# Two Strassen pairs in place of four plain output-gate blocks, and silu and the forget gate by other ScalarE functions, in a sparse-attention and gated-recurrence layer

## The chip, the core and the metric

The kernel runs on one core of a Trainium2 chip. The metric is the device time of one execution in microseconds (us); the time before is the median of three executions. All data is float32; products are made on TensorE (PE) out of high and low parts.

## The reference

One residual block over 512 tokens and 16 learned meta tokens, model width 2048. All projections come from one weight matrix `w_in` (2048 x 12368):

```
h = rms_norm(x, norm_g);  proj = h @ w_in
q_a, k_a, v_a, z_a, q_i, k_i, w_i, q_b, f_b, i_b, z_b, gates = split(proj)
# branch A: sparse attention: indexer scores, top-k keys per query, attention over them
o_a = dsa_attention(q, k, v, qi, ki, wi, chunk_ids, topk)
y_a = o_a * silu(z_a)
# branch B: gated linear recurrence, 8 heads
qb = silu(q_b);  f = lbh + (1 - lbh) * sigmoid(f_b)
o_b = rms_norm(hgrn2_chunkwise(qb, 1 - f, i_b, log(f)))
y_b = o_b * silu(z_b)
out = x + sum_n(sigmoid(gates)_n * (y_n @ w_branch_n)) @ w_out
```

## The kernel before

The program is recorded in Python: each helper of `Core` (L47 on) issues one instruction and moves a clock of its engine by an estimated cost (these clocks only decide the order). `E.tt` (L108) is a VectorE (DVE) operation on two tensors, `E.act` (L102) one on ScalarE (ACT), `E.dma_add` (L117) a DMA that adds into its target, issued by GpSimd (POOL). What is not a big product is written as generators ("tasks"). `pump` (L226) is called between matmuls and lets a task issue its next step when its operands should be ready and the clocks of DVE and ACT stand no further ahead of PE's than a limit; tasks of priority 5 or more (the top-k search and the mask table) have a limit of 1.2 us. The order on each engine is thereby fixed when the program is built, and each engine works its list in that order.

A weight tile `raw` (128x1024) comes by DMA and is split into `wh`, its rounding made on ACT, and `wl` = `raw` - `wh`, made on DVE (`hi_lo`, L399). Each product is three matmuls: high x high, high x low, low x high. There are 6 buffers for `raw` and 3 for `wh` and `wl`.

The order of the big products:

- **Class stage**: the indexer's key block, eight indexer query blocks (128 columns each), and `NZA` = 8 output-gate blocks of attention, z_a (`jobs`, L1560 on). A block is 2048 deep: 16 x 3 matmuls with 512 moving columns into the bank `pg`. Beside them run the indexer's tasks (`score`, `rl`), `tops_task` (L1199: sums of the activations for Strassen, the tiles `tr`, `t3` and `tT`), the top-k search (L679: `MAX` and `MATCH_REPLACE`, 64 rounds in all) and the mask table (`CAST`). In the last block `place_t3` (L1231) puts eight of the sums in the place of activations that were read, by an ACT copy to `hH` and a DVE difference to `hL` each.
- **Pairs**: two blocks of 128 columns are made together by Strassen's scheme with seven products (`SEVEN`, L326; `run_pair`, L1264). A product is 8 x 3 matmuls with 256 moving columns (272 in two of them where the meta tokens are needed), in the banks `px`, `py`, `px`, `pv`, `pz`, `pw`, `pz`. A pair splits 7 weight tiles; the three sums of its weights are two DVE additions `raw<-raw,raw` and two adding DMAs; six DVE operations on `p` and `r` put the two results together. The results `r0` and `r1` are finished one or two products later (`fin`). The order is 16 pairs for the recurrence (each head: forget gate with query, then value with output gate), 8 for attention, 16 for the merge gates. Beside them run one recurrence task after another (eight heads; bank `phl`, tiles `QA`, `hk`, `TT`, `attn`), and then the attention tasks.
- **Branch and output stages** follow from about 1200 us; the change leaves them as they are.

What a result waits for too long is stored to DRAM (`held`) and fetched again by a DMA that ACT issues. A z_a block is stored to `zd` and fetched as `zs` at the end of its attention head.

silu is made by a Sigmoid on ACT and a multiplication on DVE: `silu_mul` (L1112) for the blocks of the class stage, `silu` (L1136) for the recurrence's query (`qg`) and output gate (`zg`). The forget gate is a Sigmoid, then one ACT instruction that scales and shifts by the table `lbt`.

Of the kernel before, what the change touches and what calls it, by code (L numbers as in the profile page):

```python
# [12 lines left out]
AF = mybir.ActivationFunctionType  # L13
# [24 lines left out]
LAT = 180.0  # L38
SAME = {"pe": 0.0, "act": 60.0, "dve": 125.0, "pool": 60.0}
MARGIN = 300.0  # L40
NZA = 8
NSLOT = 71
ORDER = (1, 0)
LIMIT = 2000.0
# [141 lines left out]
def hybrid_kernel(ctx, tc, x, meta, vecs, w_in, rows, w_branch, w_out,  # L186
# [39 lines left out]
    def pump(limit=3000.0):  # L226
        moved = True
        while moved:
            moved = False
            for t in list(tasks):  # L230
                now = E.clk["pe"]
                lim = limit if t.prio < 5 else 1200.0
                if t.t + MARGIN <= now and E.clk["dve"] < now + lim and E.clk["act"] < now + limit:
                    if not t.done and t.step():
                        moved = True
                        break
# [235 lines left out]
    def consts():  # L472
        yield E.clk["pe"] + 3000.0
        l0, l1 = cvec[:, 16:24], cvec[:, 24:32]
        E.tt(lbt[:, :, 0], l0, l1, OP.max)
        E.tt(lbt[:, :, 1], l0, lbt[:, :, 0], OP.subtract)
        E.tt(lbt[:, :, 2], l1, lbt[:, :, 0], OP.subtract)
        yield E.act(lbt[:, :, 1:3], lbt[:, :, 1:3], AF.Exp)
        E.tt(lbt[:, :, 3], lbt[:, :, 1], lbt[:, :, 2], OP.add)
        E.dve([lbt], [lbt], 8, lambda v: v.reciprocal(lbt[:, :, 3], lbt[:, :, 3]))  # L480
        E.tt(lbt[:, :, 0], lbt[:, :, 1], lbt[:, :, 3], OP.mult)
        yield E.ts(lbt[:, :, 1], lbt[:, :, 0], -1.0, 1.0, OP.mult, OP.add)
        E.dve([gq1], [cvec], 2, lambda v: v.tensor_copy(gq1, cvec[:, 32:34]))
        E.dve([gq1], [], 2, lambda v: v.memset(gq1[0:32, :], 1.0))
        for t, o, nb in ((tabQ, 64, 4), (tabK, 128, 5)):
            E.tt(t[:, :, 0:32], tabA[:, :nb, 0:32], RB[:, None, o:o + 32].to_broadcast([128, nb, 32]), OP.mult)
            E.tt(t[:, :, 32:64], tabA[:, :nb, 32:64], RB[:, None, o + 32:o + 64].to_broadcast([128, nb, 32]),
                 OP.mult)
# [301 lines left out]
    def spill(to, s, e, n=512):  # L790
        yield e
        nc.sync.dma_start(to[:, :n], s[:, :n])
        S.put(s)
# [315 lines left out]
        yield e  # L1109


    def silu_mul(b, name):  # L1112
        s = slot(name)
        E.act(s[:, :512], b, AF.Sigmoid)
        E.tt(s[:, :512], b, s[:, :512], OP.mult)
        B1.put(b)
        return s

    def d_kiwi(b):
        s = slot("kw")  # L1120
        E.act(s[:80, :272], b[:80, 0, :272], AF.Copy)
# [11 lines left out]

    ka_tasks, va_tasks, qa_tasks, hg_tasks = {}, {}, [], []

    def silu(s, name):  # L1136
        t = slot(name)
        E.act(t[:, :512], s[:, :512], AF.Sigmoid)
        E.tt(s[:, :512], s[:, :512], t[:, :512], OP.mult)
        S.put(t)  # L1140
        return E.wr[s.tensor.name][0]

    def d_za(h):
        def f(b):
            s = silu_mul(b, "zs")
            spawn(spill(zd[h], s, E.wr[s.tensor.name][0]), 0)
        return f

    def r_za(h):
        return lambda s: spawn(spill(zd[h], s, silu(s, "zg")), 0)  # L1150

    def r_ka(g):
        def f(s):
# [11 lines left out]
    def r_qb(h):  # L1165
        def f(s):
            if h == 0:
                spawn(lb_task(), 1)
            silu(s, "qg")
            hg.setdefault(h, {})["q"] = hold(s, 512)  # L1170
        return f

# [11 lines left out]

    def r_zb(h):
        def f(s):
            silu(s, "zg")
            hg[h]["z"] = hold(s, 512)
        return f

# [63 lines left out]
    def lack_bank(n=1):  # L1254
        z = 0
        while len(B1.free) < n:
# [4 lines left out]
            if len(B1.free) < n:  # L1261
                E.clk["pe"] += 200

    def run_pair(pr, nxt, late, last):  # L1264

        bk, W, m, t = {}, slice(0, 256), pr.meta, {}
# [23 lines left out]
        for i, (wn, tn, bn, on_) in enumerate(SEVEN):  # L1290
            op = pr.ops[i]
            split_upto(op["prep"] + 2)
            if not on_:
                lack_bank()
                bk[bn] = B1.get("p" + bn)
            wide = m if bn == "x" else 0
            b = bk[bn][:, :256 + wide]
            need[0] = (2, 1, 1, 2, 1, 1, 2)[i]
            keep[0] = (2, 1, 1, 1, 1, 1, 1)[i]
            for k in range(8):  # L1300
                th, tl = TB[k][tn + "m" if wide else tn]
                st_ = k == 0 and not on_
                E.mm(b, op["h"][k], th, st_, False, loose=True)
                E.mm(b, op["h"][k], tl, False, False, loose=True)
                E.mm(b, op["l"][k], th, False, k == 7, loose=True)
                if k == WHEN:
                    flush()
                    if i == 0:
                        sum_w(pr, "s2")
                        sum_w(pr, "s1")  # L1310
                pump(LIMIT)
            if i in combine:
                pend.append(lambda f=combine[i], b=b: f(b))
            elif i == 0:
                lack()
                t["p1"] = slot("p1")
                E.act(t["p1"][:, W], b[:, wide:], AF.Copy)
            state["lazy"] = True
            split_upto(op["prep"] + 3)
            state["lazy"] = False  # L1320
            if i == 0:
                sum_w(pr, "s4")
            elif i == 2:
                lack()
                t["r0"] = slot("r0")
                E.act(t["r0"][:, :256 + m], b, f0)
                B1.put(bk["x"])
                if nxt:
                    sum_w(nxt, "s3")
            if last and i > 4:  # L1330
                flush()
            if late:
                late.pop(0)()
            if i == 5:
                def fin(s=t["r1"], f=f1, d=d1):
                    if f != AF.Copy:
                        E.act(s[:, :512], s[:, :512], f)
                    d(s)
                late.append(fin)
            elif i == 6:  # L1340
                def fin(s=t["r0"], f=f0, d=d0, m=m):
                    if f != AF.Copy:
                        E.act(s[:, m + 256:m + 512], s[:, m + 256:m + 512], f)
                    d(s)
                late.append(fin)
            if last:
                if i == 4:
                    S.put(*hH[:8], *hL[:8], *[t for k in range(8) for t in TB[k]["tiles"][:2]])
                    finish_y(ORDER[0])
# [215 lines left out]
    jobs[nclass0].pre = lambda: mask_t.append(spawn(make_masks(), 5))  # L1565
    jobs[-1].pre = lambda: sum_w(jobs[ji], "s3")
    nclass = len(jobs)
    SG, CP = AF.Sigmoid, AF.Copy
    gates = [(n, j) for n in ORDER for j in range(0, 16, 2)]

    def gate_pair():
        n, j = gates.pop(0)
        c = C_G + D * n + 128 * j
        return c, c + 128, 0, ((CP, r_gate(n, j)), (CP, r_gate(n, j + 1)))

    def za_pair(h):
        c = C_ZA + 128 * h
        return c, c + 128, 0, ((CP, r_za(h)), (CP, r_za(h + 1)))

    def attn_pairs(g):  # L1580
        return [(C_KA + 128 * g, C_QA + 256 * g, NM, ((CP, r_ka(g)), (CP, r_qa(2 * g)))),
                (C_VA + 128 * g, C_QA + 256 * g + 128, NM, ((CP, r_va(g)), (CP, r_qa(2 * g + 1))))]

    def hgrn_pairs(h):
        return [(C_FB + 128 * h, C_QB + 128 * h, NM, ((SG, r_fb(h)), (CP, r_qb(h)))),
                (C_IB + 128 * h, C_ZB + 128 * h, NM, ((CP, r_ib(h)), (CP, r_zb(h))))]

    order = [za_pair(h) for h in range(NZA, 8, 2)]
# [84 lines left out]
    for ji, job in enumerate(jobs[2:], 3):  # L1673
# [34 lines left out]
        for ch in job.chunks:  # L1708
            split_upto(ch["prep"] + 2)
            for kk_ in range(ch["nk"]):  # L1710
                kt = ch["k0"] + kk_
                if job.kind == "in":
                    mh, ml = hH[kt], hL[kt]
                else:
                    mh, ml = yH[job.n, kt], yL[job.n, kt]
                for o, c in parts:
                    mm3(o, ch, kk_, kt, mh[:, c], ml[:, c], kt == 0, kt == job.kts - 1)
                pump()
            if ji == nclass and ch["k0"] == 0:
                place_t3(0)  # L1720
                place_t3(4)
# [73 lines left out]
```

## Time and profile before

| | |
|---|---|
| time, median of 3 (lowest to highest) | 1546.42 us (1544.67 to 1546.59) |
| profiled execution: its time, its span | 1545.51 us, 1543.7 us |
| first block of the class stage with 512 columns / last four z_a blocks / pairs start | 51 us / 195 to 239 us / 239 us |
| last `MAX` of the top-k search / last `phl` matmul of the recurrence / first matmul of the branch stage | 393.3 us / 701.9 us / 1199.1 us |
| DVE busy, of the stretch from 239 to 400 us; from 400 to 700 us | 149.75 of 160.8 us; 232.75 of 300 us |

The span runs from the first instruction to the last; 1.8 us of the execution's own time lie around it. A busy PE is no PE at its peak: the records of matmuls that follow each other overlap, so what a matmul costs is read from start to start. In the timeline a row is: start, duration, engine, line, operation, tiles (out<-in), shapes, count, and in brackets the idle time of the engine before it with what ended that.

### The profile page before, as it was taken

The numbers are of one execution on the slowest core, as the hardware profiler recorded it, in microseconds if no ns is written. First come the engines' busy times: TensorE is split into PE (matmuls) and PEld (weight loads), VectorE is DVE, ScalarE is ACT, GpSimd is POOL, SyncE is SP. The second block draws the span as 40 slices with busy tenths as digits, with TensorE's granted clock in tenths as the row PEclk, the third lists the DMA queues.
The fourth block names the chain that finished last, engine by engine and source line by source line (L and its number), as shares of the span: only waits on it lengthen the run. The fifth ranks groups of instructions, "written<-read, shape, count | busy, mean of one in ns | idle before, by whom it ended". The sixth has DMA issues, their size and how long they took to land. (4 is left out here: it accounts for less than half of the span.)

```text
span 1543.7 us, 30244 instructions
## 1 busy us (share of the span) xinstructions
PE 1514.8 (98%) x12312; PEld 1425.1 (92%) x12312; DVE 1156.2 (75%) x1954; ACT 689.4 (45%) x1049; POOL 160.7 (10%) x170
## 2 busy tenths in 40 slices
PE   7999999999999999999999999999999999999998
PEld 6888889999999999999999999998999788889998
DVE  6799988999788778877776776875876444768665
ACT  5565424444443444334455455454454433434332
POOL 3100001010000101001110110110110000002221
PEclk9999999999999999999999999999999999999999
DMA  9323354787675757675775766767767664448883
GB/s 263 82 69 82 103 142 106 175 187 171 172 177 147 182 148 172 157 187 149 181 180 156 191 163 180 185 156 179 170 159 193 213 201 131 154 121 214 213 213 95
DMA packets 305563, 251.72 MB, mean 163 GB/s; under 512 B 11732, under 2 KB 266208, under 8 KB 305424
## 3 DMA queue, kind: packets, MB, share of 16 engines
q1 hardware_dynamic: 279120, 180.33, 40.1%
q0 software_dynamic: 13888, 50.42, 19.0%
q10 hardware_dynamic: 12416, 19.04, 3.9%
q8 instruction: 96, 1.57, 0.4%
q14 instruction: 43, 0.35, 0.1%
HBM read 169.90 MB, written 29.52 MB: 129 GB/s over the span
## 5 line engine op out<-in xcount | busy, mean ns | idle before, releaser
L103 ACT ACTIVATE wh<-raw 128x1024 fp32r<-128x1024 f32 x398 | 421.5, 1060 | 591.9 <-PE pz L93 137.4
L109 DVE TENSOR_TENSOR wl<-raw,wh 128x1024 fp32r<-128x1024 f32 x396 | 485.1, 1226 | 130.8 <-ACT wh L103 124.7
L118 POOL DMA_DIRECT2D raw<-raw x96 | 83.8, 980 | 1076.0 <-DVE raw L109 613.8
L93 PE MATMUL px<-hH,wh 128*128 128x272 f32 (+1 forms) x640 | 186.9, 292 | 2.7 <-ACT p L103 2.7
L93 PE MATMUL px<-hL,wh 128*128 128x272 f32 (+1 forms) x640 | 182.9, 286 | 0.0
L93 PE MATMUL px<-hH,wl 128*128 128x272 f32 (+1 forms) x640 | 182.8, 286 | 0.0
L93 PE MATMUL po<-wh,mh 128*128 128x256 f32 x896 | 159.3, 281 | 0.5 <-DVE xq L109 0.5
L93 PEld LDWEIGHTS po<-wh,mh 128*128 128x128 f32 x896 | 137.6, 189 | 0.8 <-DVE xq L109 0.7
L93 PE MATMUL po<-wl,mh 128*128 128x256 f32 x448 | 125.8, 281 | 0.0
L93 PEld LDWEIGHTS px<-hH,wh 128*128 128x128 f32 x640 | 120.8, 189 | 3.7 <-ACT p L103 3.1
L93 PE MATMUL pv<-tT,wh 128*128 128x256 f32 x640 | 121.0, 287 | 0.0
L93 PEld LDWEIGHTS px<-hL,wh 128*128 128x128 f32 x640 | 120.8, 189 | 0.0
L93 PEld LDWEIGHTS px<-hH,wl 128*128 128x128 f32 x640 | 120.6, 188 | 0.0
L93 PE MATMUL pz<-tT,wh 128*128 128x256 f32 x640 | 119.4, 286 | 0.0
L109 DVE TENSOR_TENSOR raw<-raw,raw 128x1024 f32<-128x1024 f32 x96 | 117.3, 1221 | 1.6
L93 PE MATMUL pw<-tT,wh 128*128 128x256 f32 x640 | 118.1, 284 | 0.0
L95 PE MATMUL pg<-yH,wh 128*128 128x512 f32 x256 | 101.7, 397 | 1.2 <-ACT yH L103 1.2
L95 PE MATMUL pg<-yL,wh 128*128 128x512 f32 x256 | 101.4, 396 | 1.2 <-DVE yL L109 1.2
L95 PE MATMUL pg<-yH,wl 128*128 128x512 f32 x256 | 101.6, 397 | 0.0
L93 PEld LDWEIGHTS pz<-tT,wh 128*128 128x128 f32 x640 | 99.1, 190 | 0.3
L93 PEld LDWEIGHTS pv<-tT,wh 128*128 128x128 f32 x640 | 98.1, 189 | 0.2
L93 PEld LDWEIGHTS pw<-tT,wh 128*128 128x128 f32 x640 | 97.9, 188 | 0.3
(309 smaller groups left out, 3564.4 us busy)
## 6 DMA issues: line engine op xcount, KB each, us to landing
raw<-in_w_in_dram SPq DMA_DIRECT2D x192, 512.0 KB, 6.0
raw<-raw POOLq DMA_DIRECT2D x96, 512.0 KB, 5.8
raw<-in_w_branch_dram SPq DMA_DIRECT2D x32, 512.0 KB, 4.0
raw<-in_w_out_dram SPq DMA_DIRECT2D x32, 512.0 KB, 6.4
gd<-r SPq DMA_DIRECT2D x32, 256.0 KB, 2.6
gate<-gd SPq DMA_DIRECT2D x32, 256.0 KB, 4.2
held<-r SPq DMA_DIRECT2D x20, 264.0 KB, 2.3
held<-r SPq DMA_DIRECT2D x20, 256.0 KB, 2.0
```

Source lines behind the costliest of these rows:

```text
L93: self.nc.tensor.matmul(out, lhsT, rhs, start=start, stop=stop, skip_group_check=True)
L95: self.nc.tensor.matmul(out, lhsT, rhs, start=start, stop=stop)
L103: self.nc.scalar.activation(out, in_, f, **kw)
L109: self.nc.vector.tensor_tensor(out, a, b, op=op)
L118: self.nc.gpsimd.dma_start(out, a, accum_op=OP.add)
```

## The change

- `NZA` goes from 8 to 4. Output-gate blocks 4 to 7 of attention are no more blocks of the class stage but two Strassen pairs, which stand behind the recurrence's 16 pairs and ahead of attention's.
- silu is one ACT instruction with the function Silu; the 24 multiplications on DVE (8 `zs`, 8 `qg`, 8 `zg`) are gone. For the recurrence's query and output gate the ACT instruction works in place on `r1`; for the new pairs one result is made by Silu straight from the bank, in place of a copy.
- The forget gate is made by Tanh of half the input; the table `lbt` is changed to match (one small DVE operation more).
- In the last block of the class stage `pump` has a limit of 0.5 us in place of 3.0; the limit of low-priority tasks is the smaller of 1.2 us and the caller's.

The diff, cut to its core:

```
-NZA = 8
+NZA = 4
...
-                lim = limit if t.prio < 5 else 1200.0
+                lim = limit if t.prio < 5 else min(limit, 1200.0)
...
-        yield E.ts(lbt[:, :, 1], lbt[:, :, 0], -1.0, 1.0, OP.mult, OP.add)
+        E.ts(lbt[:, :, 1], lbt[:, :, 0], -0.5, 0.5, OP.mult, OP.add)
+        yield E.ts(lbt[:, :, 0], lbt[:, :, 0], 0.5, 0.5, OP.mult, OP.add)
...
-    def silu_mul(b, name):
-        s = slot(name)
-        E.act(s[:, :512], b, AF.Sigmoid)
-        E.tt(s[:, :512], b, s[:, :512], OP.mult)
-        B1.put(b)
-        return s
...
-    def silu(s, name):
-        t = slot(name)
-        E.act(t[:, :512], s[:, :512], AF.Sigmoid)
-        E.tt(s[:, :512], s[:, :512], t[:, :512], OP.mult)
-        S.put(t)
-        return E.wr[s.tensor.name][0]
...
     def d_za(h):
         def f(b):
-            s = silu_mul(b, "zs")
+            s = slot("zs")
+            E.act(s[:, :512], b, AF.Silu)
+            B1.put(b)
             spawn(spill(zd[h], s, E.wr[s.tensor.name][0]), 0)
...
-        return lambda s: spawn(spill(zd[h], s, silu(s, "zg")), 0)
+        return lambda s: spawn(spill(zd[h], s, E.wr[s.tensor.name][0]), 0)
...
+    def silu(o, i):
+        E.act(o, i, AF.Silu)
+
+    def tanh_half(o, i):
+        E.act(o, i, AF.Tanh, scale=0.5)
...
-                E.act(t["r0"][:, :256 + m], b, f0)
+                f0(t["r0"][:, :256 + m], b)
...
-        return c, c + 128, 0, ((CP, r_za(h)), (CP, r_za(h + 1)))
+        return c, c + 128, 0, ((silu, r_za(h)), (silu, r_za(h + 1)))
...
-        return [(C_FB + 128 * h, C_QB + 128 * h, NM, ((SG, r_fb(h)), (CP, r_qb(h)))),
-                (C_IB + 128 * h, C_ZB + 128 * h, NM, ((CP, r_ib(h)), (CP, r_zb(h))))]
-
-    order = [za_pair(h) for h in range(NZA, 8, 2)]
+        return [(C_FB + 128 * h, C_QB + 128 * h, NM, ((tanh_half, r_fb(h)), (silu, r_qb(h)))),
+                (C_IB + 128 * h, C_ZB + 128 * h, NM, ((copy, r_ib(h)), (silu, r_zb(h))))]
+
+    order = []
     for h in range(8):
         order += hgrn_pairs(h)
+    order += [za_pair(h) for h in range(NZA, 8, 2)]
...
-                pump()
+                pump(500.0 if ji == nclass else 3000.0)
```

The joint between the class stage and the first pair, on DVE. The names: `hL_52` is the last of the eight differences of `place_t3`; `wl35`, `wl36`, `wl37` are the low parts of the weights for the second, third and fourth product of the first pair; `zs_252` is the multiplication for the last z_a block; `m8`, `tk` belong to the top-k search. Before:

```order
L109 TENSOR_TENSOR hL_52_406<-t3_229_1992,hH_51_405 128x256
L109 TENSOR_TENSOR wl35_2475<-raw35_2233,wh35_2474 128x1024
L688 MAX m8_120<-tk_234_2005 128x8
L689 MATCH_REPLACE tk_234_2005<-m8_120,tk_234_2005 128x400
L109 TENSOR_TENSOR zs_252_2504<-pg_98_2424,zs_252_2504 128x512
L109 TENSOR_TENSOR wl36_2508<-raw37_2312,wh36_2507 128x1024
L109 TENSOR_TENSOR raw35_2233<-raw35_2233,raw36_2275 128x1024
L109 TENSOR_TENSOR raw34_2196<-raw35_2233,raw34_2196 128x1024
L109 TENSOR_TENSOR wl37_2541<-raw35_2233,wh37_2540 128x1024
```

In the changed program the same place on DVE, where the pair's low parts are `wl26` to `wl32`; first the piece that ends with the low part for the first product:

```order
L109 TENSOR_TENSOR tT_246_2121<-tr_242_2080,tT_245_2120 128x512
L109 TENSOR_TENSOR tT_247_2122<-tr_243_2081,tT_247_2122 128x256
L321 CAST masks_100<-mf_236_2041 128x256
L692 MAX m8_120<-tk_234_2002 128x8
L693 MATCH_REPLACE tk_234_2002<-m8_120,tk_234_2002 128x528
L109 TENSOR_TENSOR wl26_2131<-raw26_1736,wh26_2130 128x1024
```

and then the piece from the last difference on:

```order
L109 TENSOR_TENSOR hL_52_406<-t3_229_1989,hH_51_405 128x256
L109 TENSOR_TENSOR wl27_2181<-raw27_1805,wh27_2180 128x1024
L321 CAST masks_100<-mf_236_2041 128x256
L692 MAX m8_120<-tk_234_2002 128x8
L693 MATCH_REPLACE tk_234_2002<-m8_120,tk_234_2002 128x528
L109 TENSOR_TENSOR wl28_2214<-raw29_1981,wh28_2213 128x1024
L109 TENSOR_TENSOR raw27_1805<-raw27_1805,raw28_1896 128x1024
L109 TENSOR_TENSOR raw26_1736<-raw27_1805,raw26_1736 128x1024
L109 TENSOR_TENSOR wl29_2247<-raw27_1805,wh29_2246 128x1024
```

What moved: the sums of the activations (`tT`), the mask table and the first rounds of the top-k search, which stood two to five blocks ahead of the first pair, now stand in its last block and in the pair itself; between `wl26` and the first `hL` there are two more rounds of mask, `MAX` and `MATCH_REPLACE`. The multiplication `zs` is gone.

The recurrence's pairs, on DVE, at the end of a forget-gate and query pair and the start of the next pair. Before (`qg` is the Sigmoid of the query; the last row gives a result of the recurrence's head, which the matmuls of `phl` wait for):

```order
L109 TENSOR_TENSOR r1_317_5059<-p1_310_4852,pw_157_5049 128x256
L109 TENSOR_TENSOR wl98_5098<-raw71_4727,wh98_5097 128x1024
L1022 COPY_PREDICATED attn_257_2752<-masks_100,phl_20_2754 128x32x8
L109 TENSOR_TENSOR hk_313_4938<-hk_313_4938,TT_316_4969 128x33x8
L109 TENSOR_TENSOR QA_315_4947<-QA_315_4947,TT_316_4969 128x32x8
L109 TENSOR_TENSOR TT_316_4969<-TT_316_4969 128x33
L109 TENSOR_TENSOR r1_317_5059<-r1_317_5059,qg_318_5149 128x512
L109 TENSOR_TENSOR r0_312_4922<-p1_310_4852,pz_156_4992 128x256
L109 TENSOR_TENSOR wl99_5147<-raw73_4902,wh99_5146 128x1024
L109 TENSOR_TENSOR raw71_4727<-raw71_4727,raw72_4900 128x1024
L109 TENSOR_TENSOR raw70_4679<-raw71_4727,raw70_4679 128x1024
L1022 COPY_PREDICATED attn_257_2752<-masks_100,phl_20_2754 128x16x16
```

And in the changed program, at the end of a pair of the same kind:

```order
L109 TENSOR_TENSOR r1_322_5378<-p1_315_5212,pw_167_5357 128x256
L109 TENSOR_TENSOR wl104_5426<-raw71_5064,wh104_5425 128x1024
L1026 COPY_PREDICATED attn_252_2454<-masks_100,phl_20_2456 128x128x2
L109 TENSOR_TENSOR hk_319_5361<-hk_319_5361,TT_323_5395 128x132x2
L109 TENSOR_TENSOR QA_321_5370<-QA_321_5370,TT_323_5395 128x128x2
L109 TENSOR_TENSOR TT_323_5395<-TT_323_5395 128x132
L109 TENSOR_TENSOR r0_317_5288<-p1_315_5212,pz_166_5324 128x256
L109 TENSOR_TENSOR wl105_5475<-raw73_5267,wh105_5474 128x1024
L109 TENSOR_TENSOR raw71_5064<-raw71_5064,raw72_5265 128x1024
L109 TENSOR_TENSOR raw70_5023<-raw71_5064,raw70_5023 128x1024
L1026 COPY_PREDICATED attn_252_2454<-masks_100,phl_20_2456 128x64x4
```

What moved: the multiplication by `qg` no longer stands ahead of the next pair's low part and sums. On ACT the Silu of `r1` stands where the Sigmoid `qg` stood.

More of the change, by code (lines that the diff above doesn't have):

```diff
@@ L275, in slot, with ready @@
         return S.get(name, dt)
+    def ready(*aps):
+        return max(E.ac.get(a.tensor.name, (0.0, ""))[0] for a in aps) + LAT
     X = {}
@@ L1168, in f @@
                 spawn(lb_task(), 1)
-            silu(s, "qg")
             hg.setdefault(h, {})["q"] = hold(s, 512)
@@ L1186, in f @@
         def f(s):
-            silu(s, "zg")
             hg[h]["z"] = hold(s, 512)
@@ L1262, in lack_bank, with copy @@
                 E.clk["pe"] += 200
+    def copy(o, i):
+        E.act(o, i, AF.Copy)
+    def silu(o, i):
+        E.act(o, i, AF.Silu)
+    def tanh_half(o, i):
+        E.act(o, i, AF.Tanh, scale=0.5)
     def run_pair(pr, nxt, late, last):
@@ L1335, in fin @@
                 def fin(s=t["r1"], f=f1, d=d1):
-                    if f != AF.Copy:
-                        E.act(s[:, :512], s[:, :512], f)
+                    if f != copy:
+                        f(s[:, :512], s[:, :512])
                     d(s)
@@ L1341, in fin @@
                 def fin(s=t["r0"], f=f0, d=d0, m=m):
-                    if f != AF.Copy:
-                        E.act(s[:, m + 256:m + 512], s[:, m + 256:m + 512], f)
+                    if f != copy:
+                        f(s[:, m + 256:m + 512], s[:, m + 256:m + 512])
                     d(s)
@@ L1567, in hybrid_kernel @@
     nclass = len(jobs)
-    SG, CP = AF.Sigmoid, AF.Copy
     gates = [(n, j) for n in ORDER for j in range(0, 16, 2)]
@@ L1573, in gate_pair @@
         c = C_G + D * n + 128 * j
-        return c, c + 128, 0, ((CP, r_gate(n, j)), (CP, r_gate(n, j + 1)))
+        return c, c + 128, 0, ((copy, r_gate(n, j)), (copy, r_gate(n, j + 1)))
     def za_pair(h):
         c = C_ZA + 128 * h
-        return c, c + 128, 0, ((CP, r_za(h)), (CP, r_za(h + 1)))
+        return c, c + 128, 0, ((silu, r_za(h)), (silu, r_za(h + 1)))
     def attn_pairs(g):
-        return [(C_KA + 128 * g, C_QA + 256 * g, NM, ((CP, r_ka(g)), (CP, r_qa(2 * g)))),
-                (C_VA + 128 * g, C_QA + 256 * g + 128, NM, ((CP, r_va(g)), (CP, r_qa(2 * g + 1))))]
+        return [(C_KA + 128 * g, C_QA + 256 * g, NM, ((copy, r_ka(g)), (copy, r_qa(2 * g)))),
+                (C_VA + 128 * g, C_QA + 256 * g + 128, NM, ((copy, r_va(g)), (copy, r_qa(2 * g + 1))))]
     def hgrn_pairs(h):
-        return [(C_FB + 128 * h, C_QB + 128 * h, NM, ((SG, r_fb(h)), (CP, r_qb(h)))),
-                (C_IB + 128 * h, C_ZB + 128 * h, NM, ((CP, r_ib(h)), (CP, r_zb(h))))]
-    order = [za_pair(h) for h in range(NZA, 8, 2)]
+        return [(C_FB + 128 * h, C_QB + 128 * h, NM, ((tanh_half, r_fb(h)), (silu, r_qb(h)))),
+                (C_IB + 128 * h, C_ZB + 128 * h, NM, ((copy, r_ib(h)), (silu, r_zb(h))))]
+    order = []
     for h in range(8):
         order += hgrn_pairs(h)
+    order += [za_pair(h) for h in range(NZA, 8, 2)]
     for g in range(4):
```

## The prediction

> **What bounds the kernel now.** The page's first part was read first, then the busy time by stretches, then the waits of PE.
>
> ```profile
> PE 1514.8 (98%) x12312; PEld 1425.1 (92%) x12312; DVE 1156.2 (75%) x1954; ACT 689.4 (45%) x1049; POOL 160.7 (10%) x170
> ...
> 195.03:239.19 44.16, 44.16 (x193) 36.06 (x192) 38.84 (x79) 13.41 (x20) 0.94 (x1) 1.00 0.43 113
> 239.20:400.00 160.80, 160.20 (x1629) 157.14 (x1628) 149.75 (x306) 69.33 (x91) 13.68 (x16) 1.00 0.70 167
> 400.00:700.00 300.00, 297.84 (x3372) 288.87 (x3371) 232.75 (x392) 124.23 (x174) 27.19 (x30) 1.00 0.69 166
> 700.00:1200.00 500.00, 487.41 (x4009) 479.18 (x4008) 354.59 (x583) 245.12 (x389) 60.25 (x70) 1.00 0.70 175
> ```
>
> In a stretch's row stand its length, then the busy time of PE, PEld, DVE, ACT and POOL. TensorE bounds every stretch: in the last four z_a blocks (195 to 239 us) it never rests, in the pairs up to 700 us it rests 0.6 + 2.16 us, and only beside attention, from 700 to 1200 us, 12.6 us. So a change can gain by less work on PE, or by these rests. Second in line is DVE: 88% busy in the z_a blocks and 93% in the first pairs, where the top-k search and the recurrence share it; after 400 us it has room (78%).
>
> ```profile
> PE px L93 <- ACT p L103: 2.7, 2, 1.3
> PE pov L93 <- ACT pT L103: 2.4, 4, 0.7
> PE pz L93 <- DVE r L109: 2.3, 3, 0.9
> PE pka L99 <- DMA xk<-held: 2.3, 1, 2.3
> PE phl L95 <- DVE QA L109: 2.2, 2, 1.1
> ...
> DVE zs L109 <- DMA zs<-zd: 18.7, 5, 4.7
> ```
>
> Of PE's waits after the start (total us, times, longest), only the one of `phl` belongs to the recurrence; `pov`, `pka` and the wait of DVE for `zs` are attention's.
>
> **Four blocks become two pairs.** The window from 195.03 to 239.19 us is exactly the last four z_a blocks: 4 x 48 matmuls in 44.16 us, 0.230 us each. A pair without meta columns is seven products of 24 matmuls with 256 columns. Such products, with no task between them, are these pieces of the chain of waits:
>
> ```profile
> 1177.91 2.85 PE px L93 x24
> 1180.76 2.85 PE py L93 x24
> 1186.46 2.83 PE pv L93 x24
> 1189.30 2.83 PE pz L93 x24
> ```
>
> Mean 2.84 us, so a pair takes 7 x 2.84 = 19.88 us and two take 39.76 us. PE does 44.16 - 39.76 = **4.4 us** less. This is the surest term: nothing else fills PE there.
>
> The weights are the same eight `raw` loads. A pair splits seven tiles and two pairs 14, against 8 for four blocks: 6 more `wh` and `wl`. It adds 4 sums on DVE, 12 combining steps and 4 adding DMAs. On DVE that is about 6 x 1.13 + 4 x 1.2 + 12 x 0.34 = 16 us (step times below), but behind the recurrence's pairs, where DVE had 22% free: nothing on PE's path. The adding DMAs
>
> ```profile
> raw<-raw POOLq DMA_DIRECT2D x96, 512.0 KB, 5.8
> ```
>
> stand in POOL's queue like the 96 others, a pair ahead of their use; the four stores to `zd` move in SP's queue from the class stage to the new pairs and stand there ahead of weight loads, as the two stores of `held` do in nearly every recurrence pair now. Both at nothing; were that cover gone, a late load would cost what it is late by, once.
>
> **The multiplications of silu.** 24 DVE steps go, and DVE no longer waits for the Sigmoid ahead of them. What that does is seen at 446 us, with the PE row that follows:
>
> ```profile
> 446.45 0.69 DVE L109 TENSOR_TENSOR r<-r,qg 128x512 f32<-128x512 f32 x1 [1.58 <-ACT qg L103]
> ...
> 448.52 2.48 DVE L109 TENSOR_TENSOR raw<-raw,raw 128x1024 f32<-128x1024 f32 x2
> ...
> 451.58 0.41 DVE L109 TENSOR_TENSOR QA<-QA,TT 128x256 f32<-128x256 f32 x1
> ...
> 452.06 0.45 PE L95 MATMUL phl<-QA,hk 128*32 128x32 f32 x16 [1.08 <-DVE QA L109]
> ```
>
> DVE idles 1.58 us for `qg`, multiplies (0.60 to the next step, half of the two `tr` further down), and the steps of the next pair push `QA` back; PE waits 1.08 us. Without the multiplication `QA` comes 2.2 us earlier, and the wait goes. The other wait of this kind (2.2 us for the two) I take as alike: a gain of **2.2 us**, between 0 (another order of the same steps brings such waits elsewhere) and 2.8 (all rests from 239 to 700 us). The next in line there is PE itself.
>
> Silu itself stands in no row. The Sigmoid of the same tile does, as the nearest:
>
> ```profile
> L103 ACT ACTIVATE zg<-r 128x512 f32<-128x512 f32 x8 | 4.9, 616 | 0.0
> L103 ACT ACT_TABLE_LOAD x4 | 5.1, 1283 | 0.8 <-PEq L1782 0.7
> ```
>
> Silu is taken at the same 0.62 us; were it twice that, 24 x 0.62 = 15 us of ACT would hide in an engine that is 45% busy. Tanh replaces Sigmoid one for one.
>
> **The joint between class stage and pairs.** Here the change takes something away. The class stage ends 44.16 us earlier, but the indexer's and `tops_task`'s work on DVE stays, so that sums, masks and top-k rounds now crowd into the last block and the first pair. From `wl25` to `wl27` DVE's list has `wl25`, two `tr` of 512 columns, four of 256, two `tT`, five rounds of mask, `MAX` and `MATCH_REPLACE`, `wl26`, eight `hL`, `wl27`. A round is what lies between the two `CAST` rows below, 1.63 us. The steps, from start to start:
>
> ```profile
> 177.32 1.02 DVE L109 TENSOR_TENSOR tT<-tr,tT 128x512 fp32r<-128x512 f32 x2
> 178.25 0.70 DVE L688 MAX8 m<-tk 128x8 f32<-128x528 f32 x1
> ...
> 179.68 1.22 DVE L109 TENSOR_TENSOR wl<-raw,wh 128x1024 fp32r<-128x1024 f32 x1
> 180.81 1.29 DVE L109 TENSOR_TENSOR tr<-hH,hL 128x512 f32<-128x512 f32 x2
> 182.01 0.70 DVE L688 MAX8 m<-tk 128x8 f32<-128x528 f32 x1
> ...
> 209.03 0.28 DVE L318 CAST masks<-mf 128x256 uint8<-128x256 f32 x1
> ...
> 210.66 0.28 DVE L318 CAST masks<-mf 128x256 uint8<-128x256 f32 x1
> ...
> 233.52 2.76 DVE L109 TENSOR_TENSOR hL<-t,hH 128x256 fp32r<-128x256 f32 x8
> 236.20 1.22 DVE L109 TENSOR_TENSOR wl<-raw,wh 128x1024 fp32r<-128x1024 f32 x1
> ...
> 240.02 0.69 DVE L109 TENSOR_TENSOR zs<-pg,zs 128x512 f32<-128x512 f32 x1 [1.45 <-ACT zs L103]
> ...
> 242.12 2.48 DVE L109 TENSOR_TENSOR raw<-raw,raw 128x1024 f32<-128x1024 f32 x2
> 244.52 1.23 DVE L109 TENSOR_TENSOR wl<-raw,wh 128x1024 fp32r<-128x1024 f32 x1
> ```
>
> Up to `wl25`, which started at 179.68 us, the two lists differ little, so that time is kept. Then: `wl25` 1.13, `tr` 1.20 and 4 x 0.335 = 1.34, `tT` 0.93, rounds 5 x 1.63 = 8.15, `wl26` 1.13, `hL` 2.68, and 1.22 for `wl27` itself: 17.8 us, so `wl27` ends at 197.5 us if DVE never idles. The first pair starts at 195.03 us. Its second product follows 3.01 us later, as in these rows, and needs the low part at its third matmul, 0.24 us on:
>
> ```profile
> 239.19 0.28 PE L93 MATMUL px<-hH,wh 128*128 128x272 f32 x1
> ...
> 242.20 0.29 PE L93 MATMUL py<-hH,wh 128*128 128x256 f32 x1
> ```
>
> That is 198.3 us: a margin of 0.8 us, where before it was 242.44 - 237.42 = 5.0 us. The third product has 0.9 us (`wl28` ends at 200.2, needed at 201.1), the fourth, after two sums and `wl29`, 0.3 us (203.8 against 204.1). DVE did idle here: 5.3 us of 44.16 in the z_a blocks. Part of that falls away with `zs` (1.45 us above). I take **1.5 us** of waits on PE, the lower part of 0 (DVE packed) to 7 us (12% idle in the first three pairs, 61 us, less the margin), since a list that is behind seldom waits.
>
> Behind the joint 58 rounds of the search are left from `wl26` on, against 45 from the corresponding `wl34` before. A round costs about 0.42 + 0.41 + 0.09 us:
>
> ```profile
> L688 DVE MAX8 m<-tk 128x8 f32<-128x272 f32 (+2 forms) x40 | 16.8, 420 | 0.1
> L689 DVE MATCH_REPLACE8 tk<-m,tk 128x272 f32<-128x272 f32 (+2 forms) x40 | 16.4, 409 | 0.0
> ```
>
> 13 more rounds are 12 us of DVE, spread over the first nine pairs; each pair loses a multiplication and a wait, 1 to 2 us. So DVE stays near the 93% that it has there now, and this costs nothing beyond the joint.
>
> **The clock.** A longer wait costs twice. At 1070 us PE had waited 2.28 us, and the stretch that follows was granted 0.60 of the clock:
>
> ```profile
> 1070.43 0.63 PE L99 MATMUL pka<-ident,xk 128*128 128x128 f32 x4 [2.28 <-DMA xk<-held]
> ...
> 1072.00:1075.40 3.40, 3.40 (x20) 3.40 (x20) 2.45 (x5) 0.00 (x0) 1.18 (x2) 0.60 1.01 250
> ```
>
> That is 3.4 x 0.4 = 1.4 us lost. The waits that I expect at the joint are single ones under 1 us, so the sum holds none of this; the slower rival below does.
>
> The Trainium skill, in "TensorE: Matmul & The Clock Gate", Part 1, puts the return to half clock after at least one idle window of about 3.4 us. By that, a wait of 2.28 us would not be punished and the slower rival would be 1.4 us better; the trace has the loss behind it, and the measurement decides.
>
> **Sum.** -4.4 (PE work) - 2.2 (`phl`) + 1.5 (joint) = -5.1 us, with attention's rests taken as they are. Against the profiled execution's own 1545.51 us that gives 1540.4 us; the median lies 0.9 us above it, so the forecast is **1541.3 us**. A measurement of this kernel can tell about 0.2%, 3.1 us, from no change; faster means below 1543.3 us.
>
> **Rivals.**
> 1. *DVE's list at the joint is later than I count.* For it: 88% busy now, margins of 0.3 to 0.9 us. Against: `zs` and its wait go. At 5.5 us of waits the time is 1545.3 us, no change. Chance 0.14.
> 2. *Attention's rests change.* Its tasks run beside other products than before. A third of the 12.6 us more or less, 4 us: 1545.3 or 1537.3 us, 0.08 each. For it: waits of 0.7 to 2.3 us by chance of order; against: the steps are the same, and `zs` is fetched as late as before.
> 3. *Slower.* DVE keeps idling 12% while behind, PE waits 7 us in the first three pairs, one wait passes 2.28 us and costs 1.4 us of clock, and the `phl` waits come back elsewhere: -4.4 + 7 + 1.4 = +4, about 1550.5 us. It decides once the waits exceed 4.4 + 3.1 = 7.5 us. Chance 0.12.
> 4. *The change does not do what it says*: Silu and Tanh need different tables, and ACT reloads at every alternation, about four times a head: 32 x 1.28 = 41 us on ACT, in the recurrence's pairs, each load ahead of a `wh`; that eats the gain, 1546 us. Against: the built program holds four table loads as before, at the corresponding places. Chance 0.04.
>
> The Trainium skill's "ScalarE: Activation LUTs", Table sets, lets functions of one set alternate freely and counts about 2.7 us for a switch; it lists Tanh beside sigmoid, and Silu nowhere. By its figure rival 4 would cost ACT twice as much; no trace so far shows Silu.
>
> **How the numbers follow.** Forecast 0.54 (its own range 1538.5 to 1544; 0.46 of it below 1543.3), rivals 0.14, 0.16, 0.12, 0.04. Faster: 0.46 + 0.08 = 0.54. Same: 0.08 + 0.14 + 0.08 + 0.04 = 0.34. Slower: 0.12. The range 1536 to 1548 leaves out the slower rival and a little of the lower end.
>
> **What would show it.** In the changed profile: the two pairs behind the recurrence take 39.8 us plus what tasks stand between; the row of PE's wait for `QA` is gone or under 1 us; between 195 and 260 us PE waits for `wl` or `hL` for 0 to 3 us; table loads are four; attention's rests stay at 10 to 15 us. Wrong would be: waits over 5 us at the joint, or a `phl` wait that returns in other pairs.

## The result, and the profile after

The changed kernel took **1534.56 us** (median of 6, 1534.10 to 1538.30) beside 1546.02 us (1544.67 to 1547.11) for the kernel before on the same chip: ratio 0.9932 [0.9922, 0.9942], 11.5 us less where 5.1 were forecast. Measured again later (`e18` below) it took 1534.90 us.

The profiled execution took 1537.39 us and spans 1535.6 us. It is one of the slower ones: its pairs start at 198.26 us, in the profile of `e18` at 196.1 us; from 20 to 51 us TensorE was granted 0.92 of the clock, `e18` 0.99 and the kernel before 1.00. First its stretches, in the columns of the prediction:

```profile
198.26:222.31 24.05, 20.97 (x169) 20.38 (x168) 23.78 (x44) 8.46 (x10) 2.44 (x3) 1.00 0.60 140
400.00:700.00 300.00, 300.00 (x3365) 290.82 (x3354) 233.09 (x400) 125.28 (x179) 28.38 (x32) 1.00 0.65 160
584.16:633.53 49.37, 49.37 (x567) 47.89 (x566) 38.21 (x64) 20.34 (x29) 4.54 (x5) 1.00 0.66 161
700.00:1192.00 492.00, 486.09 (x4018) 479.52 (x4016) 352.02 (x572) 243.40 (x381) 55.25 (x67) 1.00 0.71 176
1131.13:1151.05 19.92, 19.92 (x170) 19.92 (x169) 12.97 (x14) 8.08 (x9) 1.73 (x2) 1.00 0.83 198
```

The first row is the first pair: 24.05 us, of which PE rests 3.1. From 400 to 700 us PE no longer rests (2.16 us before). The two new pairs (584 to 634 us) hold tasks of the recurrence as well; a pair of the same form without tasks takes 19.92 us (last row). From 700 us to the branch stage PE rests 5.9 us, where it rested 12.2 up to that point (12.6 up to 1200 us).

PE's waits of the changed kernel (total us, times, longest):

```profile
PE pz L93 <- DVE r L109: 2.3, 2, 1.4
PE py L93 <- DVE wl L109: 2.0, 1, 2.0
PE pg L95 <- DVE yL L109: 2.0, 2, 1.2
PE px L93 <- ACT p L103: 1.3, 1, 1.3
PE pov L93 <- ACT pT L103: 0.9, 3, 0.5
...
PE pg L95 <- ACT yH L103: 0.9, 1, 0.9
...
PE pka L99 <- DMA xk<-held: 0.8, 1, 0.8
```

With the smaller ones (0.6 us for `hk`, 0.2 for another `wl`, 0.2 for `pqa<-xq`) all rows of the view come to 11.2 us, those of before to 16.0, where the waits of the first stage (`pc`, `px<-xm`, `pg<-el`) and of the output stage (`po`) are left out in both. `phl<-QA` is gone, the joint's `py<-wl` is new, and `pka`, `pqa`, `px` and `pov` have become 5.4 us less. This sum of rows is used for every kernel below; the rests over 0.25 us that the expectations speak of are counted from start to start, and are a little larger (12.9 and 16.7 us).

### The profile page after: what moved, and what is told of

Same layout as the page of the kernel before. It is cut to its first block, busy times and chain, and to the rows that moved or that the text cites. A ratio compares the mean times of both kernels' runs of the same rounds, so it can differ in the third digit from the quotient of the medians.

```text
span 1535.6 us, 30559 instructions
## 1 busy us (share of the span) xinstructions
PE 1509.5 (98%) x12456; PEld 1427.7 (93%) x12456; DVE 1158.5 (75%) x1951; ACT 696.2 (45%) x1059; POOL 161.5 (11%) x174
## 3 DMA queue, kind: packets, MB, share of 16 engines
q0 software_dynamic: 14464, 52.52, 19.7%
## 4 chain that ended last, share of the span: by engine, by line
PE 89%; DVE 6%; DMA 2%; issue 1%; ACT 1%; POOL 0%; ACTq 0%; SPq 0%; DVEq 0%; POOLq 0%
PE pg L95 18%; PE px L93 15%; PE pz L93 14%; PE po L93 10%; PE pv L93 7%; PE py L93 7%; PE pw L93 7%; DVE wl L109 2%; PE phl L95 1%; PE pov L93 1%; PE psc L95 1%; PE plg L95 1%; PE pho L95 1%; DVE tk L693 1%; PE px L99 1%
## 5 line engine op out<-in xcount | busy, mean ns | idle before, releaser
L103 ACT ACTIVATE wh<-raw 128x1024 fp32r<-128x1024 f32 x404 | 427.9, 1060 | 570.6 <-PE pz L93 138.8
L109 DVE TENSOR_TENSOR wl<-raw,wh 128x1024 fp32r<-128x1024 f32 x402 | 493.1, 1227 | 136.7 <-ACT wh L103 133.6
L93 PE MATMUL px<-hH,wh 128*128 128x272 f32 (+1 forms) x672 | 194.5, 289 | 1.3 <-ACT p L103 1.3
L93 PE MATMUL px<-hH,wl 128*128 128x272 f32 (+1 forms) x672 | 191.9, 286 | 0.0
L93 PE MATMUL px<-hL,wh 128*128 128x272 f32 (+1 forms) x672 | 191.9, 286 | 0.0
L93 PEld LDWEIGHTS px<-hH,wh 128*128 128x128 f32 x672 | 126.7, 189 | 2.1 <-ACT p L103 1.6
L93 PEld LDWEIGHTS px<-hL,wh 128*128 128x128 f32 x672 | 126.8, 189 | 0.0
L93 PEld LDWEIGHTS px<-hH,wl 128*128 128x128 f32 x672 | 126.6, 188 | 0.0
L93 PE MATMUL pw<-tT,wh 128*128 128x256 f32 x672 | 126.4, 287 | 0.0
L93 PEld LDWEIGHTS pw<-tT,wh 128*128 128x128 f32 x672 | 103.0, 189 | 0.2
```

What stands on the lines that cost most here:

```text
L93: self.nc.tensor.matmul(out, lhsT, rhs, start=start, stop=stop, skip_group_check=True)
L103: self.nc.scalar.activation(out, in_, f, **kw)
L109: self.nc.vector.tensor_tensor(out, a, b, op=op)
```

## Experiments

Theory A: the shorter DVE list of the new functions brings the gains of the recurrence and of attention. B: attention's gain comes from where the two new pairs stand. C: PE's rests depend on how the lists happen to fall, and nearly any edit deals them anew. D: the change itself takes the rests away, whatever the list. All times are medians; each ratio is against the kernel before on the same chip.

### One part at a time (e1, e2)

`e1` is the kernel before with Silu and Tanh; the blocks and `pump` stay (the diff is against the changed kernel, as all that follow):

```
-NZA = 4
+NZA = 8
...
-                pump(500.0 if ji == nclass else 3000.0)
+                pump()
```

> The kernel before with Silu and Tanh alone (eight z_a blocks stay in the class stage). By start-to-start times of PE the profiled executions differ by: pair work -4.4 us, joint of class stage and first pair +3.9, the rest of the recurrence's pairs -4.4, attention's stretch up to the branch stage -6.8, a later start +3.1. Theory A (the thinner DVE list brings the gains of both the recurrence and attention): 1546.0 - 4.4 - 6.8 = about 1535 us. Theory B (attention's gain comes from where the two new pairs stand, the recurrence's from the functions): about 1541.6 us, attention's rests near 18 us as before. Theory C (attention's rests are a matter of how the list happens to fall, and differ with every change of it): recurrence -4.4, attention's rests anywhere from 11 to 18 us, 1535 to 1542 us.

Measured: 1543.32 us, ratio 0.9983 [0.9974, 0.9992], just above C's range. `e2` is the changed kernel with the old functions (the core of the edit; the query, all output gates and the forget gate go back to Sigmoid):

```
-        E.act(o, i, AF.Silu)
+        E.act(t[:, :512], s[:, :512], AF.Sigmoid)
+        E.tt(s[:, :512], s[:, :512], t[:, :512], OP.mult)
```

> The changed kernel with silu again as Sigmoid and a DVE multiplication, and the forget gate as Sigmoid: the two pairs alone. Theory A (functions carry both gains): -4.4 + 3.9 or more at the joint (the DVE list is longer by one multiplication of 0.7 us and its wait of 1.4), 1546 us or a little more. Theory B (place of the pairs): -4.4 + 3.9 - 6.8, about 1538.7 us. Theory C: 1539 to 1546 us, with attention's rests that fit neither before nor after.

Measured: 1553.33 us, ratio 1.0050 [1.0038, 1.0062], slower than each theory allowed. Alone, the parts give -2.8 and +7.2 us (before: 1546.11 us on that chip); together they give -11.5. A and B, by which one part brings the gain and keeps it, fall. PE's waits of `e1`, then of `e2`:

```profile
PE pka L99 <- DMA xk<-held: 2.4, 2, 1.7
PE pqa L99 <- DMA xq<-held: 1.7, 1, 1.7
```

```profile
PE px L93 <- ACT p L103: 4.0, 3, 1.4
PE pz L93 <- DVE r L109: 3.1, 4, 0.9
PE pv L93 <- DVE pTM L109: 3.1, 1, 3.1
PE phl L95 <- DVE QA L109: 2.7, 4, 1.1
PE phl L99 <- DMA v<-held: 2.6, 3, 1.3
```

`e1` has no row of `phl` for `QA`, `e2` has 2.7 us: that part follows the functions. Most of the other rows are of attention, the combining steps and fetched results, whose instructions neither edit changes; with them it is 13.6 us of waits in all in `e1`, 23.9 in `e2`.

### The place of the pairs (e3) and the joint (e4)

```
-    order = []
+    order = [za_pair(h) for h in range(NZA, 8, 2)]
...
-    order += [za_pair(h) for h in range(NZA, 8, 2)]
```

> The changed kernel with its two output-gate pairs ahead of the recurrence's pairs in place of behind them. Theory B: attention's tasks stand beside the same products as before, its 6.8 us are lost, about 1541.4 us. Theory A: no change, 1534.6 us (the joint may be a little better, since the recurrence does not yet load DVE there). Theory C: attention's rests at a third value, 1532 to 1541 us.

Measured: 1554.28 us, ratio 1.0056 [1.0043, 1.0069], above every expectation, C's too: 22.8 us of waits. But it shows a new pair with no task beside it:

```profile
219.00:238.90 19.90, 19.90 (x171) 19.90 (x169) 19.57 (x31) 8.83 (x11) 1.72 (x2) 1.00 0.76 177
```

`e4` holds the search back from the last class block to the end of the first pair:

```
+                if t.prio == 6 and quiet[0]:
+                    continue
...
         if ji == nclass:
+            quiet[0] = True
...
             run_pair(job, None if last else jobs[ji], late, last)
+            quiet[0] = False
```

> The changed kernel with no round of the top-k search in the last class block and the first pair; the rounds come later, beside the recurrence. My account of the joint: some eleven rounds of 1.4 us stand in DVE's list between the low parts and push them late, PE waits 2.0 + 0.2 + 0.9 us (3.9 us start to start). Without them these waits go: about 1531 us if the later pairs take the rounds for nothing. Rival: the later pairs pay it back, since DVE is 93 to 95% busy up to 400 us: 1534.5 us and waits for wl or r between 225 and 300 us.

Measured: 1542.25 us, ratio 0.9976 [0.9966, 0.9986]. The first pair of `e4`:

```profile
195.15:215.40 20.25, 20.25 (x170) 20.21 (x169) 13.55 (x15) 8.59 (x10) 2.29 (x3) 1.00 0.75 169
```

20.25 us without a rest, against 24.05: the rounds were the cause of the joint's 3.8 us. The other profiles agree: the first pair takes 23.6 to 24.3 us in all nine with the new pairs and the search not held, 20.2 in those with it held (20.7 in `e17`), and 20.2 in the six kernels with eight blocks. Yet the kernel became 7.7 us slower. The rival of e4's expectation is not it either (no wait for `wl` later on): its waits are other ones again, 2.4 us for `xk`, 1.9 for `v`, 1.9 for `pT`.

### The same instructions in other lists (e5 to e8, e13, e14)

`MARGIN` only says how long operands must have been ready, by the estimate, before a task goes on. One line:

```
-MARGIN = 300.0
+MARGIN = 280.0
```

> The changed kernel with the number MARGIN 280 in place of 300: how many ns a task's operands must have been ready, by the estimate, before it issues its next step. The same instructions are issued, some thousands of them in other places of their lists. Theory C (attention's rests are a matter of how the list falls): the time moves by several us either way, the sum of PE's rests over 0.25 us from the first pair to the branch stage anywhere from 13 to 29 us (12.9 in the changed kernel), 1535 to 1550 us. Theory D (the change itself takes these rests away): within 2 us of 1534.6, rests of 11 to 15 us.

> The changed kernel with MARGIN 320 in place of 300. Theory C: another value between 1535 and 1550 us, rests of 13 to 29 us. Theory D: within 2 us of 1534.6.

> The kernel before with MARGIN 280 in place of 300. Theory C: it moves by several us as well, 1538 to 1552 us; rests over 0.25 us from the first pair to the branch stage (16.7 in the kernel before) from 12 to 25 us. Theory D: within 2 us of 1546.

> The kernel before with MARGIN 320 in place of 300. Theory C: another value between 1538 and 1552 us. Theory D: within 2 us of 1546. With the two runs of the changed kernel: if the change is worth the 4 to 5 us that its own terms give (-4.4 pair work, -2.2 to -4.4 recurrence, +3.9 joint), the mean of the three changed kernels lies 3 to 5 us below the mean of the three of before.

> The changed kernel with MARGIN 260. Theory C: 2 us below the kernel before with MARGIN 260, plus or minus 7 us; 1536 to 1550 us by itself. Theory D: 11 us below it. Its joint waits 3 to 4 us in either.

> The kernel before with MARGIN 260. Theory C: 1540 to 1551 us, no wait at the joint. Theory D: 1546 us.

| MARGIN | before: us | changed: us | difference |
|---|---|---|---|
| 260 | 1550.49, ratio 1.0026 [1.0015, 1.0037] | 1551.23, 1.0035 [1.0021, 1.0048] | +0.7 |
| 280 | 1543.96, 0.9988 [0.9979, 0.9996] | 1543.70, 0.9987 [0.9978, 0.9995] | -0.3 |
| 300 | 1545.7 | 1534.56, 0.9932 [0.9922, 0.9942] | -11.1 |
| 320 | 1542.80, 0.9978 [0.9969, 0.9987] | 1546.94, 1.0006 [0.9997, 1.0015] | +4.1 |

(1545.7 us is the median of 34 executions of the kernel before on the chip of the runs with 280 and 320; on the changed kernel's own chip the difference is -11.5.) D falls: with the three other numbers the change is worth nothing or less. The changed kernels with 260 and 320 wait in attention where the one with 300 does not; the largest rows of 260:

```profile
PE pv L93 <- DVE pTM L109: 3.6, 1, 3.6
PE pqa L99 <- DMA xq<-held: 3.6, 3, 1.9
PE ppt L99 <- DVE p L109: 3.2, 1, 3.2
...
PE py L93 <- DVE wl L109: 2.1, 1, 2.1
```

and of 320:

```profile
PE pka L99 <- DMA xk<-held: 2.8, 2, 2.2
PE pz L93 <- DVE r L109: 2.5, 3, 1.1
PE py L93 <- DVE wl L109: 2.1, 1, 2.1
```

The joint's `py<-wl` is the same in all three (2.0, 2.1, 2.1): with the first pair's length above, a property of the change. Such rows as `pTM` or `xk` are the list's.

### Fetched results (e9 to e12)

PE waits for `held` 1.0 us in the changed kernel, and 2.6 to 6.8 us in all others so far. The planner takes 4 us for such a fetch. How `z` came in `e5`, with its last line the time from issue to landing:

```profile
L801 ACTq DMA_DIRECT2D z<-held x7: 446/466/872, 316.6 to 685.4; - x7
...
DMA to landing us min/median/max: 2.9/5.9/9.4
```

So the estimate was raised:

```
-        E.wr[s.tensor.name] = (E.clk["pe"] + 4000.0, "dma")
+        E.wr[s.tensor.name] = (E.clk["pe"] + 7000.0, "dma")
```

> The changed kernel where the estimate for a fetched result, by which its task waits before it issues its next step, is 7 us in place of 4. The fetches from held, q, f, v, z, xk, xq, xv and zs, landed after 1.9 to 9.4 us in the traces so far, and PE, DVE and ACT lists wait in order for those that are later than planned. Theory C1 (a good part of the rests that differ from list to list are such late fetches): PE's rows that wait for held, 1.0 us here and up to 6.5 us in the neighbours, and DVE's for zs and q are gone or under 0.5 us, and the time is at or below 1534.6 us, 1530 to 1536, since the changed kernel had few of them. Theory C2 (the fetches are only one of many chances): another draw of the list, 1538 to 1547 us like the two neighbours with another MARGIN.

> The kernel with the search held back at the joint (1542.25 us) and the estimate of 7 us for fetched results. C1: its rows that wait for held (5.1 us) and the half clock behind the 2.4 us one (1.4 us) go, the joint stays without a wait: 1535 us or less, down to 1527 us if the rows of pqa for qay and of pov go with them. C2: 1538 to 1547 us.

> The kernel before with an estimate of 6 us for fetched results in place of 4. C1: PE's 3.5 us for held, the 1.4 us of half clock behind the longest of them, and DVE's 18.7 us for zs go, the last with what PE loses by it: 1537 to 1542 us, so that a part of the 11.5 us is to be had without the change. C2: 1540 to 1549 us, no clear difference from 1545.7.

> The changed kernel with an estimate of 6 us for fetched results, the counterpart of the kernel before with 6 us (1551.2 us). The three pairs so far with the same numbers in both kernels (MARGIN 300, 280, 320) differ by -11.1, -0.3 and +4.1 us, mean -2.4. Theory C with a worth of the change itself of about -2 us (-4.4 pair work, -1.5 waits for QA, +3.7 joint) and lists that scatter by some 5 us: 1549 us, anywhere from 1541 to 1557. Theory D (the change is worth 11 us): 1540 us.

Measured: `e9` 1550.12 us, 1.0036 [1.0023, 1.0048]; `e10` 1534.71, 0.9931 [0.9919, 0.9944]; `e11` 1551.20, 1.0046 [1.0032, 1.0060]; `e12` 1544.16, 0.9983 [0.9974, 0.9993]. The rows for `held` did go (0, 0, 0 and 0.4 us), but C1 holds for `e10` only. In `e9` this stands in their place, with ACT's timeline behind it:

```profile
PE pg L95 <- ACT yH L103: 6.8, 1, 6.8
PE plg L95 <- ACT qH L103: 4.0, 1, 4.0
```

```profile
1185.99 1.06 ACT L103 ACTIVATE wh<-raw 128x1024 fp32r<-128x1024 f32 x1 [9.99 <-DMA yr<-yd]
1200.02 1.30 ACT L103 ACTIVATE gate<-gate 128x512 f32<-128x512 f32 x2 [6.57 <-DMA gate<-gd]
```

Tasks that wait 3 us longer at each fetch end later, so that attention's last steps (the last `plg` at 1212.8 us, in the changed kernel at 1109.4) now stand in the branch stage, behind ACT's waits for that stage's own loads. One wait was turned into another. With `e11`, `e12` is a further pair with the same number, on two chips: -7.0 us.

### Lists with few waits (e15 to e17), and the changed kernel again (e18)

`e15`: the search held as in `e4`, the estimate 6 us, MARGIN 360. `e16`: 6 us, MARGIN 280, LIMIT 1500. `e17`: 5.5 us, MARGIN 240, LIMIT 2500. The numbers were chosen out of some sixty by adding up rows' durations along each engine's list, so these three are no blind draws.

> The kernel with the search held back at the joint, an estimate of 6 us for fetched results and MARGIN 360: a list in which the rests that differ from list to list should be few. Theory C: without the joint's 3.7 us and with no more rests from the first pair to the branch stage than the changed kernel has outside the joint (8 us), about 1531 us, the lowest so far; 1528 to 1538. If the joint or the fetches don't matter beside other chances, 1538 to 1547 us.

> The search held back at the joint, an estimate of 6 us for fetched results, MARGIN 280 and LIMIT 1500 (how far DVE's and ACT's planned clocks may stand ahead of PE's in a pair): a second list of the kind of the one that took 1534.05 us. Theory C: no wait at the joint, no row for held over 0.5 us, 1528 to 1538 us like it. If that one was a lucky list of a kind that scatters like the others, 1536 to 1548 us.

> The same with an estimate of 5.5 us, MARGIN 240 and LIMIT 2500: a third list of that kind, 1528 to 1538 us, or 1536 to 1548 us if the kind scatters.

> The changed kernel once more, unchanged, beside the two others on the same chip: 1534.6 us by the first measurement. Its profile tells what of the first one's execution (3.1 us late at the first class block, 2.0 us of wait at the joint, full clock behind that wait and at the start of the branch stage) belongs to the list and what to that execution: the waits at the same places, the clock possibly not.

Measured: `e15` 1534.05 us, 0.9920 [0.9907, 0.9934]; `e16` 1537.77, 0.9949 [0.9936, 0.9961]; `e17` **1532.10** (1530.70 to 1532.59), 0.9909 [0.9895, 0.9922]; `e18` 1534.90 (1534.36 to 1537.44), 0.9931 [0.9918, 0.9945]. `e17` lies below both kernels, and 2.8 us below the changed one on the same chip, with no overlap. Its largest waits:

```profile
PE pz L93 <- DVE r L109: 1.5, 2, 0.8
PE pg L95 <- ACT yH L103: 1.5, 1, 1.5
PE pov L93 <- ACT pT L103: 1.5, 3, 0.5
```

With the smaller ones they are 6.7 us, the fewest of all kernels. `e18` repeats most waits of the changed kernel's first profile, 10.1 us in all against 11.2:

```profile
PE py L93 <- DVE wl L109: 1.8, 1, 1.8
...
PE px L93 <- ACT p L103: 1.3, 1, 1.3
```

So the waits belong, in the main, to the list and come again in another execution; they are not noise.

### All kernels together

Each profile's span less its own sum of waits (sum of rows as above):

| | span | waits | span less waits |
|---|---|---|---|
| before, e1, e7, e8, e11, e14 (eight z_a blocks) | 1539.4 to 1549.4 | 11.8 to 19.7 | 1525.7 to 1530.4, mean 1528.6 |
| changed, e18, and the other twelve (two new pairs) | 1530.0 to 1550.3 | 6.7 to 23.9 | 1520.6 to 1527.4, mean 1524.3 |

Without its waits a kernel with the pairs is 4.3 us shorter, give or take 2.0 (95%, from the scatter in the last column): that agrees with the 4.4 us of PE's work. With them, 6.7 to 23.9 us decide the rest.

## Why the prediction was wrong, step by step

The sign and the surest term were right, the sum was not: 1541.3 us, 1536 to 1548, against 1534.56. The step that failed is "with attention's rests taken as they are": they and their clock became 7.9 us less. The joint was mis-sized the other way, 3.9 us for 1.5.

**Pair work, -4.4: right.** 19.9 us for a pair (row of `e3`), 19.88 taken; -4.3 us over all kernels.

**silu, -2.2: right in kind, some 1.6 us in size.** The `phl<-QA` rows are 2.2, 1.4, 0.9, 1.2, 2.1 and 2.7 us in the six kernels with the multiplications, mean 1.75, and 0 to 0.8, mean 0.2, in the fourteen profiles without. `e1` alone measured -2.8 us, but with other waits in it as well, so that this agreement proves little. Silu's cost and the tables were as taken:

```profile
L103 ACT ACTIVATE r<-r 128x512 f32<-128x512 f32 x18 | 11.1, 615 | 0.0
...
L103 ACT ACT_TABLE_LOAD x4 | 5.1, 1283 | 0.8 <-PEq L1781 0.7
L103 ACT ACTIVATE zs<-pg 128x512 f32<-128x512 f32 x4 | 2.4, 598 | 8.2 <-PE pg L95 8.1
```

Rival 4 is out.

**The joint, +1.5: mis-sized, +3.8.** The DVE list of the changed kernel there:

```profile
185.72 1.21 DVE L109 TENSOR_TENSOR wl<-raw,wh 128x1024 fp32r<-128x1024 f32 x1
...
188.26 0.70 DVE L692 MAX8 m<-tk 128x8 f32<-128x528 f32 x1
...
191.35 0.71 DVE L692 MAX8 m<-tk 128x8 f32<-128x528 f32 x1
...
193.91 0.70 DVE L692 MAX8 m<-tk 128x8 f32<-128x528 f32 x1
...
196.67 0.71 DVE L692 MAX8 m<-tk 128x8 f32<-128x528 f32 x1
...
198.30 0.70 DVE L692 MAX8 m<-tk 128x8 f32<-128x528 f32 x1
...
199.72 2.76 DVE L109 TENSOR_TENSOR hL<-t,hH 128x256 fp32r<-128x256 f32 x8
202.40 1.22 DVE L109 TENSOR_TENSOR wl<-raw,wh 128x1024 fp32r<-128x1024 f32 x1
```

and PE's:

```profile
201.40 0.28 PE L93 MATMUL py<-hL,wh 128*128 128x256 f32 x1
203.67 0.39 PE L93 MATMUL py<-hH,wl 128*128 128x256 f32 x1 [2.00 <-DVE wl L109]
...
219.40 0.36 PE L93 MATMUL pz<-hH,wh 128*128 128x256 f32 x1 [0.86 <-DVE r L109]
```

From the start of `wl25` (185.72 us) to the end of `wl27` (203.62) it is 17.9 us, with five rounds: the sum of 17.8 us was exact. What failed is the step ahead of it, "the two lists differ little" up to `wl25`. That starts 6.0 us later than before, and the pairs 3.2 us later than the 195.03 that the sum used: 2.8 us too late against PE, so the margin of 0.8 became a wait of 2.0. The trace shows what made it late: from 155 to 180 us DVE waits 3.9 us, in the kernel before 1.4. The longest of these waits is for an `rl` that ACT, by the profile, makes only when the store of a z_a block has landed:

```profile
172.08 0.58 ACT L103 ACTIVATE rl<-psc 128x144 f32<-128x144 f32 x2 [5.32 <-DMA zd<-zs]
172.40 0.79 DVE L132 SCALAR_TENSOR_TENSOR score<-rl,wi,score 128x144 f32<-128x144 f32 x2 [2.46 <-ACT rl L103]
```

Every profile with Silu has this wait (2.1 to 2.6 us), `e1` too; none with the multiplications has it. It comes with the new functions, not with the pairs. One search round more (1.4 us) also stands ahead of `wl25`, and a multiplication `zs` (0.6 us) is gone. The wait alone is not the joint's price: `e2` is without it, and its first pair takes 23.6 us by other waits. In the first pair DVE did not idle, as the upper bound of 7 us took it to: it is 99% busy there. Rival 1 had the place; its 5.5 us were more than the 3.1 of waits.

**Attention's rests taken unchanged: this step failed.** Waits shrank by 4.8 us in all (16.0 to 11.2), although the joint added 3.1 of them; what of the clock was lost at 1070 us (1.7 us) went with the wait for `xk`. By the rests the two profiles nearly add up: -4.4 us of work, +3.9 at the joint (24.05 us for the first pair, 20.18 before), -2.2 from 400 to 700 us, -6.2 beside attention and -1.7 of clock make -10.6, of 11.5 measured. Rival 2 named this, with a third of 12.6 us as its price and a chance of 0.16 for both signs. But it is no matter of "other products" beside the tasks: a `MARGIN` of 280 or 320 does it too, and moves the kernel before by up to 7.7 us between lists (1542.80 to 1550.49), the changed one by 16.7 (1534.56 to 1551.23). A stretch in which PE, 98% busy, waits in order for three other engines and for DMAs has rests that no edit here left alone; they should have had a scatter of some 5 us in the sum, of both signs.

What the change is worth by itself: -4.4 - 1.6 + 3.8 = -2.2 us. The five pairs of kernels with the same numbers (+0.7, -0.3, -11.1, +4.1, and -7.0 with the estimate of 6 us) have a mean of -2.7 us, with a 95% interval of about -10 to +5 (standard deviation 6.2 us over five): in keeping with it, and with no change. The other nine of the 11.5 us come with the list that this edit happened to make: numbers that change only the list take them away. Why this list has so few late fetches, no run shows.

Of the signs named to look for, the 19.9 us of a pair, the four table loads and the missing `QA` row came true; waits at the joint (3.1 us) just passed their 0 to 3, and attention's rests (5.9 us) missed their 10 to 15.

**The slower rival**, 1550.5 us, did not come, but `e2`, `e3`, `e9` and `e13` show that an edit of this kind lands there as easily.

## What to carry to other kernels

Where one engine is nearly always busy and the order of its work is fixed when the program is built, an edit has two effects: its own, and a new deal of all waits behind it. Before a gain is put down to the edit, change a number that should not matter, in both kernels, and see how far the time moves by that; the sum of the engine's wait rows, taken off the span, shows the edit's own part with less scatter (6.8 us from lowest to highest among the kernels with the new pairs, where the spans differ by 20.3). And what holds for a list holds for tuning: the lists can be chosen, and here that was worth 2.8 us beyond the changed kernel (`e17`), about what the change is worth by itself.

## What the runs showed of the hardware

**The same wait costs a slower clock once and not another time.** The clock (third figure from the end) behind the joint's wait of 2.00 us in the changed kernel, then in `e18`, the same program, behind 1.81 us, then in `e2` behind 3.07 us:

```profile
203.67:207.07 3.40, 3.40 (x28) 3.40 (x29) 3.37 (x6) 0.00 (x0) 0.00 (x0) 1.00 0.00 0
```

```profile
201.00:203.00 2.00, 1.73 (x10) 1.73 (x11) 1.97 (x6) 0.00 (x0) 0.00 (x0) 0.70 0.00 0
203.00:205.10 2.10, 2.10 (x12) 2.10 (x12) 2.10 (x2) 0.00 (x0) 0.00 (x0) 0.50 0.00 0
```

```profile
1124.02:1127.42 3.40, 3.40 (x25) 3.26 (x26) 3.33 (x8) 1.51 (x4) 0.00 (x0) 1.00 1.08 235
```

Length does not decide: behind 3.07 us the clock stayed full, and 1.81 us brought half clock, 0.50, from 203.0 to 205.1 us. The Trainium skill, in "TensorE: Matmul & The Clock Gate", Part 1, has a window of some 3.4 us that runs freely, not from the kernel's start. That would let the same wait fall into it differently in two executions, and the traces agree so far; that a whole idle window is needed they do not bear out. What share of a window is enough, no run here shows. The price that the prediction put on a wait over 2.28 us is thus a chance, not a rule. Its size was read a little low: the clock was at 0.79 from 1070.43 to 1072.00 us already, so that 1.7 us were lost there, not 1.4. At the joint the slower clock cost nothing: the first pair took 23.87 us in `e18`, 24.05 in the changed kernel's first profile, since the later waits for DVE (0.22 and 0.86 us) are missing in `e18`.

**A fetch of 256 KB took 2.9 to 9.4 us** in one execution (`z` in `e5` above): the planner's 4 us lies well below the median of 5.9.
